# Down-projection of a seven-product gated MLP: another bank order, weight sums moved into the sweep, the last sums issued behind the next norm

## The chip, the cores and the metric

The kernel is one program on one core of a Trainium2 chip. TensorE multiplies matrices into PSUM (eight banks of 128 x 512 float32), VectorE and ScalarE do elementwise work and read PSUM, GpSimd works on SBUF alone, and SyncE issues all the transfers here. Each engine runs its own queue in order, and engines wait for each other by semaphores. The metric is the device time of one execution in microseconds. The times shown are those of three runs and, apart from them, of one profiled execution.

## The reference

A two-layer decoder over 1024 positions of width 1024, all in float32. Each layer has a mixer and a gated MLP (`conv_ffn`) of inner width 2816; the first mixer is a recurrence with a state-space layer, the second is latent attention (`mla`).

```python
for layer in range(2):
    hn = rmsnorm(h, norm_mix_g[layer])
    h = h + (even_mixer(hn, ...) if layer % 2 == 0 else mla(hn, positions, ...))
    h = h + conv_ffn(rmsnorm(h, norm_ffn_g[layer]), ffn_w_in[layer], ffn_conv_w[layer],
                     ffn_conv_b[layer], ffn_w_out[layer])
return rmsnorm(h, final_norm_g)

def conv_ffn(hn, w_in, conv_w, conv_b, w_out):
    a, u = jnp.split(hn @ w_in, 2, axis=-1)
    a = causal_depthwise_conv_width_3(a, conv_w) + conv_b
    return (jax.nn.silu(a) * u) @ w_out
```

The change touches the end of `conv_ffn` and the norm and first projections of `mla`.

## The kernel before, in words

Every float32 product is made of three fast ones: both operands are split into a high part (ScalarE, line 130) and a remainder (VectorE, line 131), and `mm3` (lines 162 to 164) adds high times high, and the two mixed ones.

Both matrix products of the MLP are done by a scheme of Strassen's kind: the operands are cut into halves along rows and columns, sums and differences of these are formed, and seven products of half size take the place of eight.

**The sweep** (`ffn`). The inner width is swept in 22 column blocks of 128, numbered `f`. Each has seven products of 12 matmuls (12 = 4 slices of the inner dimension x 3), which go to three banks X, Y and Z of the block; from the third block on, banks are drawn in turn from a list (`bank()`, list 3, 0, 6, 4, 1, 7, 5, 2). ScalarE and VectorE read the banks between the products (`run`, `tail`); L914 and L935 are the VectorE reads of the product in Y and of the last one in Z. GpSimd forms the sums of the raw weights (L883 to L889). The gated result of each block, `ct`, is stored to DRAM (`g_dram`).

Blocks go in pairs, `q` = 0 to 10. After the second block of a pair, `tail` puts steps on the list `later`: four `row_sums` (sums of the pair's results, stored to `g_dram`) and, up to the last pair but one, a set of `weight_sums` of the same pair: two loads of 128 x 1024 of the output weights, three empty steps, four subtractions (L985), each stored to `t_dram` (L986). One step is taken after each product of the sweep. Both kinds work in the same two tiles (`homes`: q1 has the place of `gain`, q2 that of the last of three `wlo` tiles). The last pair's set and what is left are issued in `between`, after the first product of the down-projection.

**The down-projection** (`down`). Seven products of 132 matmuls each: 11 pairs `q` x 4 row blocks `t` x 3. Each product accumulates into four banks, one for a row block. X is the first four banks of the ring (0 to 3), Y the other four; later products reuse them. For each `q` a *unit* is made: a row tile is loaded (L1150 from `g_dram`, L1155 from `t_dram` or from the weights), then split on ScalarE and VectorE into one of the unit buffers: six pairs of halves in the places of the MLP's operands and four tiles of its own pool, 14 in all, or 10 for the last product, which leaves two large places free for the next norm. Row tiles go round ten places, one of them the place of q2. Units are asked for nine ahead. The last `tail` values of `q` are done row block by row block, so that the four banks end one after the other. `add` (L1180) then adds each bank to the residual rows `h`; each product feeds one or more quarters of `h`. The last product, number 6, feeds the second half's right quarter; the rows of the first half are complete one product earlier.

**The border to the attention layer** (`mla`). `norm_rows` squares the rows on ScalarE (L201), takes the reciprocal root on VectorE (L173 to L184, ten small operations for two rows), scales the rows (L205), transposes them on TensorE (L211, tiles `tps`) into banks tagged `t`, and splits them into `hn`. The low-rank projections (tile `low`) follow, with banks tagged `mm`. In the second MLP, `final` norms and stores each row block as it is completed.

**What sets the order.** The program is written in Python's order and a scheduler lays each engine's queue from a simulated timeline; `high_priority` and `issue_after` (an instruction issued no sooner than a given one) shape it. On the chip the queues stand as laid.

Of the kernel before, what the change touches and what calls it, by code (L numbers as in the profile page):

```python
# [27 lines left out]
NF = FF // P  # L28
# [14 lines left out]
HM = 5  # L43
FRAW, FW = 2, 0
LOOK = 3
EL, OL = (1, 2), (1, 3)
LASTMAJ, MB, FB = True, (2, 2), (1, 2)
SEQ = "s s k00 s s g0 s q00 r00 k02 r01 q02 s r02 s v1 r03 s o0 g1 s k10 q10 r10 k12 q12 r11 r12 r13"
# [8 lines left out]
class Trunk:  # L57
# [134 lines left out]
    def norm_rows(self, h, g, batch=4, tags=("hn", "hn")):  # L192

        nc = self.nc
        hi = self.slot(tags[0], [P, KD, HALF], F32R, name="hn_hi")
        lo = self.slot(tags[1], [P, KD, HALF], F32R, name="hn_lo")
        ss = self.small.tile([P, TB], F32, tag="ss", name="ss")
        for b0 in range(0, TB, batch):
            for t in range(b0, b0 + batch):
                junk = self.xp.tile([P, D], F32, tag=self.xtag, name="junk", bufs=2)  # L200
                nc.scalar.activation(junk, h[:, t], AF.Square, accum_out=ss[:, t:t + 1])  # L201
            r = self.rstd(ss[:, b0:b0 + batch], D, batch)
            for t in range(b0, b0 + batch):
                xn = self.xp.tile([P, D], F32, tag=self.xtag, name="xn", bufs=2)
                nc.vector.scalar_tensor_tensor(  # L205
                    out=xn, in0=h[:, t], scalar=r[:, t - b0:t - b0 + 1], in1=g, op0=ALU.mult, op1=ALU.mult
                )
                for q in range(2):
                    ps = self.bank(name="tps", tag="t")
                    for k in range(4):  # L210
                        nc.tensor.transpose(  # L211
                            ps[:, k * P:(k + 1) * P], xn[:, (4 * q + k) * P:(4 * q + k + 1) * P], self.ident
                        )
                    dst = lambda x: x[:, 4 * q:4 * q + 4, t * P:(t + 1) * P]
                    self.split(dst(hi), dst(lo), ps.rearrange("p (k n) -> p k n", k=4))
        return hi, lo
# [605 lines left out]
    def ffn(self, L, h, pool, final=None):  # L822


        nc, tc = self.nc, self.tc
        V, G, ACT = nc.vector, nc.gpsimd, nc.scalar
        self.xp, self.xtag = pool, "ct"
        w_in, w_out = self.a["ffn_w_in"][L], self.a["ffn_w_out"][L]
# [4 lines left out]
        g_dram, t_dram = (  # L833
            tc.dram_tile([NF // 2, n, P, HALF], F32, name=name) for n, name in ((7, "g_dram"), (4, "t_dram"))
        )
        KH = KD // 2
        last, later = [], []
        quad = [P, 2, KH, HALF]
        piece = lambda name, bufs: pool.tile([P, HALF], F32, tag=name, name=name, bufs=bufs)
        kn = lambda x: x.rearrange("p (k n) -> p k n", k=KH)  # L840
# [92 lines left out]
        def tail(p):  # L933
            ct = p.ct
            V.tensor_tensor(out=p.p16, in0=p.p16, in1=p.Z, op=ALU.add)  # L935
            V.tensor_tensor(out=ct[:, lo], in0=ct[:, lo], in1=p.X, op=ALU.mult)
            G.tensor_tensor(out=ct[:, hi], in0=ct[:, hi], in1=p.p16, op=ALU.mult)
            q, odd = p.f // 2, p.f % 2
            put = lambda i, x: nc.sync.dma_start(out=g_dram[q, i], in_=x)
            put(odd, ct[:, hi])  # L940
            if not odd:
                return
            put(2, ct[:, lo])
            later.extend(row_sums(q, pairs[p.f - 1].ct, ct))
            if p.f < NF - 1:
                later.extend(weight_sums(q))

        def homes():
            return (
# [24 lines left out]
        def weight_sums(q):  # L974

            x = []

            def load():
                for i, y in enumerate(homes()):
                    nc.sync.dma_start(out=y, in_=w_out[(2 * q + i) * P:(2 * q + i + 1) * P])  # L980
                    x.extend((y[:, lo], y[:, hi]))

            def step(i, out, a, b):
                def go():
                    V.tensor_tensor(out=x[out], in0=x[a], in1=x[b], op=ALU.subtract)  # L985
                    nc.sync.dma_start(out=t_dram[q, i], in_=x[out])  # L986
                return go

            wait = lambda: None
            return [load, wait, wait, wait, step(0, 0, 1, 0), step(2, 1, 3, 1), step(1, 3, 3, 0), step(3, 2, 2, 3)]  # L990

        two = lambda tag, name: (lambda v: (v[:, 0], v[:, 1]))(self.slot(tag, quad, F32R, name=name))
        single = lambda tag, name, dtype=F32R: pool.tile([P, KH, HALF], dtype, tag=tag, name=name, bufs=1)
# [97 lines left out]
        for i, (p, name) in enumerate(steps):  # L1091
            if i + LOOK < len(steps):
                prep(*steps[i + LOOK])
            for x, first in (("X", "a11"), ("Y", "s2"), ("Z", "s1")):
                if name == first:
                    setattr(p, x, here(p.banks[x]) if p.f < 3 else bank())
            run(p, name)
            if later:
                later.pop(0)()
            left[p.f] -= 1  # L1100
            if not left[p.f]:
                tail(p)

        self.psum(mm=8)
        later.extend(weight_sums(NF // 2 - 1))

        def between():
            while later:
                later.pop(0)()
            return final() if final is not None else None  # L1110

        self.down(h, g_dram, t_dram, w_out, between)

    def conv(self, out, ax, taps, f, span):

# [6 lines left out]
            nc.vector.scalar_tensor_tensor(out=t, in0=at(s), scalar=col(s), in1=t, op0=ALU.mult, op1=ALU.add)  # L1122
        nc.scalar.activation(t, t, AF.Silu)

    def down(self, h, g, turned, w, between):


        nc, tc = self.nc, self.tc
        V = nc.vector
        nq = NF // 2  # L1130
        low = [(x, n) for tag, k in (("hn", 2), ("g", 3)) for x in [tag] * k for n in range(2)]
        own = [(f"b{i}", 0) for i in range(2, 6)]
        units = {True: low + own, False: low[4:] + own}
        held, at, last = {}, [0], []

        def unit(free):
# [24 lines left out]
        def product(banks, a, b, start, free, tail):  # L1161
            us = []
            order = [(q, t) for q in range(nq - tail) for t in range(TB)]
            order += [(q, t) for t in range(TB) for q in range(nq - tail, nq)]
            for q, t in order:
                while len(us) < min(nq, q + 9):
                    us.append(operands(len(us), a, b, free))
                u = us[q]
                with tc.issue_after(last[0].ins) if last else nullcontext():
                    mm = self.mm3(  # L1170
                        banks[t], [u[:, i, 0, t * P:(t + 1) * P] for i in range(2)], [u[:, i, 1] for i in range(2)],
                        start and q == 0, q == nq - 1, skip_group_check=not start,
                    )
                last[:] = [mm]

        def add(banks, *to, done=()):
            for t in range(TB):
                for half, col in to:
                    x = h[half][:, t, col * HALF:(col + 1) * HALF]
                    V.tensor_tensor(out=x, in0=x, in1=banks[t], op=ALU.add)  # L1180
                for half, col in done if final is not None else ():
                    final(h[half], half, t, col)
# [12 lines left out]
        X = banks()  # L1195
# [2 lines left out]
        product(Y, 2, 3, False, True, 3)  # L1198
        add(Y, (0, 0), done=[(0, 0), (0, 1)])
        at[0] = 0  # L1200
        product(X, 6, (1, 1), False, False, 7)
        add(X, (1, 1), done=[(1, 1)])

    def project_rows(self, h, x, w, tags=("mm",) * TB, late=1):

# [101 lines left out]
        nc.gpsimd.tensor_tensor(out=d[:, :, 0], in0=pc[:, :, 0], in1=ps[:, :, 1], op=ALU.subtract)  # L1307
        nc.vector.tensor_tensor(out=d[:, :, 1], in0=pc[:, :, 1], in1=ps[:, :, 0], op=ALU.add)

    def mla(self, h, keep, pool):  # L1310
        nc, tc, a = self.nc, self.tc, self.a
        NT = S // P
        w_in = a["odd_w_in"][0]
# [3 lines left out]
        ka = keep.tile([P, S], F32R, name="ka", bufs=1)  # L1317
        kb = keep.tile([P, S], F32R, name="kb", bufs=1)
        with pool("mla_in") as tp, self.weights(0, 5, 768), pool("norm", "right") as self.xp:
            self.psum(mm=6, t=2)  # L1320
            self.xtag = "xn"
            g_row = self.gain(a["norm_mix_g"][1:2])
            gains = {}
# [4 lines left out]
            for half in range(2):  # L1328
                with tc.high_priority():
                    tags = ("hn", "hn") if half == 0 else ("h", "g")  # L1330
                    hn.append(self.norm_rows(h[half], g_row, batch=MB[half], tags=tags))
                    for t in range(TB):
                        nc.sync.dma_start(out=spill[half][:, t], in_=h[half][:, t])
            cos, sin = self.rope_tables(tp)
            cq = [self.slot("g", [P, QR // P, S], F32R, name=n) for n in ("cq_hi", "cq_lo")]
            ck = self.slot("h", [P, 2, KVR // P, S], F32R, name="ckv")
# [291 lines left out]
def trunk(tc, a, out, parts=("mix0", "ffn0", "mix1", "ffn1")):  # L1628
    with ExitStack() as ctx:
        T = Trunk(ctx, tc, a, out)  # L1630
        pool = lambda n, side="left": tc.tile_pool(name=n, bufs=2, reuse_waits="tile", side=side)
        first_g = []
        start = lambda: first_g.append(T.gain(a["norm_mix_g"][0:1])) if parts[0] == "mix0" else None
        h = [T.load_rows(0, start), None if parts[0] == "mix0" else T.load_rows(1)]
        for part in parts:
            if part == "mix0":
                T.psum(mm=4, s5=1, s5p=1, t=2)
                with T.weights(), pool("hgrn") as hp:
                    h = T.even(h, first_g[0], hp, pool, lambda n: pool(n, "right"), lambda: pool("mix_out"))
            elif part == "mix1":  # L1640
                with pool("mla") as keep:
                    h = T.mla(h, keep, pool)
            else:
                L = int(part[3])
                T.psum(mm=6, t=2)
                with T.weights(FRAW, FW), pool(part, "right") as fp:
                    T.ffn(L, h, fp, final=(lambda: T.final(fp)) if part == parts[-1] else None)


INS = [  # L1650
# [24 lines left out]
```

## Time and profile before

| | us |
|---|---|
| median of three runs (2300.55 to 2304.01) | 2301.92 |
| profiled execution | 2303.47 |
| its span, first to last instruction | 2301.8 |
| TensorE busy in it | 2206.0 |
| VectorE busy | 1648.9 |
| ScalarE busy | 925.4 |
| GpSimd busy | 553.7 |

Mean granted TensorE clock: 0.985 of full speed. The first MLP's sweep runs from about 485 to 913, its down-projection to 1136, the attention layer to about 1620, the second MLP's sweep from there to 2069 and its down-projection to 2293. In what follows PE is TensorE, PEld its weight loads, DVE VectorE, ACT ScalarE, POOL GpSimd and SP SyncE. A wait is idle time of an engine, put down to the instruction that ended it.

### The profile page before, as it was taken

The numbers are of one execution on the slowest core, as the hardware profiler recorded it, in microseconds if no ns is written. First come the engines' busy times: TensorE is split into PE (matmuls) and PEld (weight loads), VectorE is DVE, ScalarE is ACT, GpSimd is POOL, SyncE is SP. The second block draws the span as 40 slices with busy tenths as digits, with TensorE's granted clock in tenths as the row PEclk, the third lists the DMA queues.
The fourth block names the chain that finished last, engine by engine and source line by source line (L and its number), as shares of the span: only waits on it lengthen the run. The fifth ranks groups of instructions, "written<-read, shape, count | busy, mean of one in ns | idle before, by whom it ended". The sixth has DMA issues, their size and how long they took to land. (4 is left out here: it accounts for less than half of the span.)

```text
span 2301.8 us, 30062 instructions
## 1 busy us (share of the span) xinstructions
PE 2206.0 (96%) x10681; PEld 1815.2 (79%) x10681; DVE 1648.9 (72%) x2749; ACT 925.4 (40%) x1564; POOL 553.7 (24%) x509
## 2 busy tenths in 40 slices
PE   7999999999999999899799999999999999999998
PEld 6777887877777887788698888888777878877786
DVE  6778896698777777654467677766887777777556
ACT  4454544443333334342243555544533333333432
POOL 0365510125444442100001000000344444431000
PEclk9999999999999999999999999999999999999999
DMA  6432333415444446864311001054144444558642
GB/s 188 136 99 87 99 92 109 139 37 173 152 148 159 146 164 228 288 201 131 128 31 43 28 22 39 29 179 137 37 156 160 141 166 136 180 197 293 206 155 82
DMA packets 257214, 306.18 MB, mean 133 GB/s; under 512 B 35680, under 2 KB 159784, under 8 KB 256552
## 3 DMA queue, kind: packets, MB, share of 16 engines
q1 hardware_dynamic: 257064, 304.26, 40.2%
q8 instruction: 84, 1.38, 0.3%
q14 instruction: 66, 0.54, 0.1%
HBM read 223.06 MB, written 79.95 MB: 132 GB/s over the span
## 5 line engine op out<-in xcount | busy, mean ns | idle before, releaser
L162 PE MATMUL au<-bt,op 128*128 128x512 f32 x704 | 280.8, 399 | 15.7 <-DVE p L914 8.5
L131 DVE TENSOR_TENSOR unit<-row,unit 128x1024 fp32r<-128x1024 f32 x154 | 185.5, 1233 | 149.2 <-ACT unit L130 136.8
L163 PE MATMUL au<-bt,op 128*128 128x512 f32 x704 | 278.9, 396 | 1.2 <-DVE bt L131 1.2
L164 PE MATMUL au<-bt,op 128*128 128x512 f32 x704 | 278.8, 396 | 0.0
L130 ACT ACTIVATE op<-raw 128x512 fp32r<-128x512 f32 x260 | 161.7, 627 | 254.2 <-PE au L164 123.3
L162 PE MATMUL row<-unit 128*128 128x512 f32 x616 | 243.8, 396 | 18.4 <-ACT unit L130 10.3
L130 ACT ACTIVATE unit<-row 128x1024 fp32r<-128x1024 f32 x154 | 155.6, 1053 | 255.6 <-PE row L164 166.9
L131 DVE TENSOR_TENSOR op<-raw,op 128x512 fp32r<-128x512 f32 x260 | 217.3, 838 | 56.7 <-ACT op L130 56.3
L163 PE MATMUL row<-unit 128*128 128x512 f32 x616 | 243.2, 395 | 2.1 <-DVE unit L131 2.1
L164 PE MATMUL row<-unit 128*128 128x512 f32 x616 | 242.8, 394 | 0.0
L164 PE MATMUL au<-b,op 128*128 128x512 f32 x528 | 208.6, 395 | 1.1 <-DVE op L131 1.1
L162 PE MATMUL au<-b,op 128*128 128x512 f32 x528 | 208.5, 395 | 0.0
L163 PE MATMUL au<-b,op 128*128 128x512 f32 x528 | 208.4, 395 | 0.0
L162 PEld LDWEIGHTS au<-bt,op 128*128 128x128 f32 x704 | 132.6, 188 | 56.2 <-DVE p L914 14.0
L131 DVE TENSOR_TENSOR wlo<-raw,whi 128x1024 fp32r<-128x1024 f32 (+4 forms) x99 | 118.1, 1194 | 62.5 <-ACT whi L130 61.8
L163 PEld LDWEIGHTS au<-bt,op 128*128 128x128 f32 x704 | 132.9, 189 | 32.5 <-DVE bt L131 1.5
L164 PEld LDWEIGHTS au<-bt,op 128*128 128x128 f32 x704 | 132.8, 189 | 31.9
L130 ACT ACTIVATE whi<-raw 128x1024 fp32r<-128x1024 f32 (+4 forms) x99 | 96.7, 980 | 141.9 <-PE row L164 63.2
L162 PEld LDWEIGHTS row<-unit 128*128 128x128 f32 x616 | 117.6, 191 | 45.0 <-ACT unit L130 11.2
L163 PEld LDWEIGHTS row<-unit 128*128 128x128 f32 x616 | 117.6, 191 | 28.5 <-DVE unit L131 3.5
L164 PEld LDWEIGHTS row<-unit 128*128 128x128 f32 x616 | 117.3, 190 | 25.0
L883 POOL TENSOR_TENSOR s<-raw 128x512 f32<-128x512 f32 x44 | 63.1, 1436 | 267.1 <-DMA raw<-in_ffn_w_in 231.8
(599 smaller groups left out, 5081.5 us busy)
## 6 DMA issues: line engine op xcount, KB each, us to landing
raw<-in_ffn_w_in SPq DMA_DIRECT2D x176, 256.0 KB, 3.4
row<-g_dram SPq DMA_DIRECT2D x154, 256.0 KB, 4.0
g_dram<-q SPq DMA_DIRECT2D x88, 256.0 KB, 3.7
q<-in_ffn_w_out SPq DMA_DIRECT2D x44, 512.0 KB, 4.1
t_dram<-q SPq DMA_DIRECT2D x88, 256.0 KB, 2.1
row<-t_dram SPq DMA_DIRECT2D x88, 256.0 KB, 4.2
raw<-in_even_w_in SPq DMA_DIRECT2D x40, 512.0 KB, 3.7
g_dram<-ct SPq DMA_DIRECT2D x66, 256.0 KB, 2.1
```

Source lines behind the costliest of these rows:

```text
L130: nc.scalar.activation(hi, src, AF.Copy)
L131: nc.vector.tensor_tensor(out=lo, in0=src, in1=hi.bitcast(F32), op=ALU.subtract)
L162: mm(out, l[0], r[0], start=start, stop=False, **how)
L163: mm(out, l[0], r[1], start=False, stop=False, **how)
L164: return mm(out, l[1], r[0], start=False, stop=stop, **how)
L883: tt(out=s.s1, in0=p("a21"), in1=p("a22"), op=ALU.add)
```

## The change

Four edits, for both MLPs unless said:

- The down-projection's banks come from a list, 0, 4, 1, 6, 7, 5, 2, 3, instead of 0 to 7. The attention layer's norm and projections take their banks from lists, too.
- Sets of weight sums are put on the list after blocks 5, 7, 9 (two), 11, 13 (two), 15, 17 (two) and 19, all eleven of them in the sweep; each ends with one more empty step, and two steps are taken after a product while more than 14 wait.
- Units are asked for as far ahead as there are buffers less one. The last product of the first MLP has only the six units in the large places, and its last three values of `q` are done row block by row block instead of the last seven.
- The last product's `add` is handed back as a function. In the second MLP it is called at once; in the first it is called inside the attention layer, after the norm of the first half, and not ahead of that norm's last scaling.

```diff
+TURNS = {5: 1, 7: 1, 9: 2, 11: 1, 13: 2, 15: 1, 17: 2, 19: 1}
...
-                nc.vector.scalar_tensor_tensor(
+                self.scaled = nc.vector.scalar_tensor_tensor(
...
             later.extend(row_sums(q, pairs[p.f - 1].ct, ct))
-            if p.f < NF - 1:
-                later.extend(weight_sums(q))
+            for _ in range(TURNS.get(p.f, 0)):
+                later.extend(weight_sums(turned[0]))
+                turned[0] += 1
...
-            return [load, wait, wait, wait, step(0, 0, 1, 0), step(2, 1, 3, 1), step(1, 3, 3, 0), step(3, 2, 2, 3)]
+            return [load, wait, wait, wait, step(0, 0, 1, 0), step(2, 1, 3, 1), step(1, 3, 3, 0), step(3, 2, 2, 3), wait]
...
-            if later:
-                later.pop(0)()
+            for _ in range(1 + (len(later) > 14)):
+                if later:
+                    later.pop(0)()
...
-        self.psum(mm=8)
-        later.extend(weight_sums(NF // 2 - 1))
+        self.rings = {"mm": [[0, 4, 1, 6, 7, 5, 2, 3], 0]}
...
-        units = {True: low + own, False: low[4:] + own}
+        units = {True: low + own, False: low[4:] + (own if last_layer else [])}
...
-                while len(us) < min(nq, q + 9):
+                while len(us) < min(nq, q + len(units[free]) - 1):
...
-        product(X, 6, (1, 1), False, False, 7)
-        add(X, (1, 1), done=[(1, 1)])
+        product(X, 6, (1, 1), False, False, 7 if last_layer else 3)
+        return lambda: add(X, (1, 1), done=[(1, 1)])
...
-            self.psum(mm=6, t=2)
+            self.rings = {"mm": [[2, 3, 0, 4, 1, 6], 0], "t": [[7, 5], 0]}
...
                     for t in range(TB):
                         nc.sync.dma_start(out=spill[half][:, t], in_=h[half][:, t])
+                if half == 0:
+                    with tc.issue_after(self.scaled.ins):
+                        rest()
```

The queue of transfers (SP) at the start of the first MLP's down-projection, around the last row sums, before. `q` tiles are the two homes, L980 and L986 the loads and stores of a weight set:

```order
L964 DMA g_dram<-q_7900 128x512
L980 DMA q_7909<-in_ffn_w_out 128x1024
L1150 DMA row<-g_dram 128x512 x2
L1155 DMA row<-in_ffn_w_out 128x512
L980 DMA q_7910<-in_ffn_w_out 128x1024
L986 DMA t_dram<-q_7909 128x512
L1150 DMA row<-g_dram 128x512
L1155 DMA row<-in_ffn_w_out 128x512
```

The same place now, after the last row sum (lines have moved by two to four):

```order
L966 DMA g_dram<-q_7912 128x512
L1154 DMA row<-g_dram 128x512
L1159 DMA row<-in_ffn_w_out 128x512
L1154 DMA row<-g_dram 128x512
L190 DMA gain<-in_norm_mix_g 128x1024
L1154 DMA row<-g_dram 128x512
L1159 DMA row<-t_dram 128x512
```

The weight set that stood between the row loads is gone; the next thing on this queue that is no row load is the gain of the next norm.

VectorE's queue at the border, before: `h<-h,row` are the additions, `v` and `vy` the reciprocal root of the norm:

```order
L1180 TENSOR_TENSOR h<-h,row 128x512
L131 TENSOR_TENSOR unit<-row,unit 128x1024 x4
L1180 TENSOR_TENSOR h<-h,row 128x512 x4
L173 TENSOR_SCALAR v _9166<-ss 128x2
L1271 TENSOR_TENSOR ang<-freq,pos 128x8x32
L174 TENSOR_SCALAR vy<-v _9166 128x2
```

And now, from the end of the first half's norm on (`wlo` are weights of the projections, `hn_lo` the transposed rows):

```order
L206 SCALAR_TENSOR_TENSOR xn<-h,vy,gain 128x1024 x2
L132 TENSOR_TENSOR wlo<-raw,whi 128x640
L1184 TENSOR_TENSOR h<-h,row 128x512
L132 TENSOR_TENSOR wlo<-raw,whi 128x640
L1184 TENSOR_TENSOR h<-h,row 128x512
L132 TENSOR_TENSOR hn_lo<-tps,hn_hi 128x4x128
L1184 TENSOR_TENSOR h<-h,row 128x512
L132 TENSOR_TENSOR hn_lo<-tps,hn_hi 128x4x128
L1184 TENSOR_TENSOR h<-h,row 128x512
L174 TENSOR_SCALAR v _9271<-ss 128x2
```

The four additions of the last product stood ahead of the whole norm; they stand behind the first half's last scaling now, and ahead of the second half's root.

TensorE's queue at the end of the last product (`row<-unit`) before:

```order
L162 MATMUL row<-unit 128x512
L163 MATMUL row<-unit 128x512
L164 MATMUL row<-unit 128x512
L211 MATMUL tps<-ident,xn 128x128 x8
L162 MATMUL low<-whi,hn_hi 128x384
L163 MATMUL low<-wlo,hn_hi 128x384
```

And now, 51 matmuls into that product:

```order
L163 MATMUL row<-unit 128x512
L164 MATMUL row<-unit 128x512
L165 MATMUL row<-unit 128x512
L212 MATMUL tps<-ident,xn 128x128 x8
L163 MATMUL row<-unit 128x512
L164 MATMUL row<-unit 128x512
L165 MATMUL row<-unit 128x512
```

The first transposes of the norm stood behind the whole product; three of the first half's four groups of eight stand inside it now, after 51, 85 and 121 of its 132 matmuls.

## Rows read from the trace of the kernel before

**Rows 1.** Page, span and part 1: busy us, share of the span, instructions

```profile
span 2301.8 us, 30062 instructions
PE 2206.0 (96%) x10681; PEld 1815.2 (79%) x10681; DVE 1648.9 (72%) x2749; ACT 925.4 (40%) x1564; POOL 553.7 (24%) x509
```

**Rows 2.** Windows: length, busy (instructions) by engine, PEclk, DMA share, GB/s

```profile
910.00:920.00 10.00, 6.69 (x29) 5.16 (x28) 8.33 (x9) 7.83 (x9) 0.83 (x1) 1.00 1.03 376
965.00:985.00 20.00, 13.12 (x45) 9.91 (x45) 7.92 (x8) 5.69 (x6) 0.00 (x0) 0.74 0.69 239
990.00:1090.00 100.00, 100.00 (x442) 82.63 (x441) 48.91 (x47) 34.64 (x34) 0.53 (x2) 1.00 0.53 173
2065.00:2080.00 15.00, 10.20 (x34) 7.83 (x34) 12.42 (x12) 11.33 (x13) 2.04 (x2) 0.77 0.91 327
2125.00:2140.00 15.00, 10.34 (x33) 7.64 (x32) 6.48 (x7) 5.17 (x5) 0.00 (x0) 0.77 0.77 245
```

**Rows 3.** Windows of 5 us at the border to the attention layer

```profile
1135.00:1140.00 5.00, 0.83 (x4) 0.36 (x2) 2.42 (x8) 0.00 (x0) 0.00 (x0) 1.00 0.57 183
1140.00:1145.00 5.00, 0.00 (x0) 0.00 (x0) 4.16 (x15) 1.15 (x2) 0.00 (x0) 0.58 0.55 157
1145.00:1150.00 5.00, 1.72 (x8) 1.57 (x8) 4.29 (x7) 1.91 (x4) 0.00 (x0) 0.50 0.47 131
1150.00:1155.00 5.00, 4.00 (x17) 3.71 (x16) 3.14 (x9) 4.97 (x10) 0.00 (x0) 0.55 0.45 131
...
1180.00:1185.00 5.00, 1.20 (x12) 0.99 (x10) 5.00 (x24) 1.08 (x2) 0.00 (x0) 1.00 0.00 2
1185.00:1190.00 5.00, 4.43 (x16) 4.13 (x15) 4.71 (x16) 1.13 (x2) 0.00 (x0) 0.52 0.32 105
1190.00:1195.00 5.00, 5.00 (x29) 4.96 (x29) 1.21 (x2) 1.09 (x2) 0.00 (x0) 0.80 0.00 0
```

**Rows 4.** TensorE's waits, 885 to 1210: total us, times, longest

```profile
PE tps L211 <- DVE xn L205: 16.3, 2, 12.5
PE row L162 <- ACT unit L130: 6.4, 1, 6.4
PE row L162 <- DVE p L935: 3.3, 1, 3.3
```

**Rows 5.** TensorE's waits, 2060 to 2302

```profile
PE row L162 <- DVE p L935: 4.8, 1, 4.8
PE row L162 <- ACT unit L130: 3.9, 1, 3.9
```

**Rows 6.** Timeline of the DMA queue: start, us, queue, line, transfer

```profile
949.79 0.33 SPq L986 DMA_DIRECT2D t_dram<-q  x1
...
962.33 1.46 SPq L986 DMA_DIRECT2D t_dram<-q  x1
963.84 2.63 SPq L1155 DMA_DIRECT2D row<-t_dram  x2
```

**Rows 7.** Timeline of VectorE at the border

```profile
1135.87 0.69 DVE L1180 TENSOR_TENSOR h<-h,row 128x512 f32<-128x512 f32 x1 [4.13 <-PE row L164]
1136.47 0.16 DVE L173 TENSOR_SCALAR v _9166<-ss 128x2 f32<-128x2 f32 x1
...
1146.95 2.48 DVE L205 SCALAR_TENSOR_TENSOR xn<-h,vy,gain 128x1024 f32<-128x1024 f32 x2
```

**Rows 8.** Timeline of ScalarE at the border

```profile
1112.17 1.04 ACT L201 ACTIVATE junk<-h 128x1024 f32<-128x1024 f32 x1
```

**Rows 9.** Window: the first 110 us of the first sweep

```profile
500.00:610.00 110.00, 104.64 (x444) 82.43 (x443) 91.39 (x109) 33.48 (x52) 52.61 (x42) 1.00 0.46 151
```

**Rows 10.** VectorE's groups, 500 to 900: busy us, mean ns, idle before

```profile
L985 DVE TENSOR_TENSOR q<-q,q 128x512 f32<-128x512 f32 x20 | 18.8, 940 | 0.9 <-DMA q<-in_ffn_w_out 0.9
...
L985 DVE TENSOR_TENSOR q<-q 128x512 f32<-128x512 f32 x20 | 14.3, 714 | 34.0 <-DMA q<-in_ffn_w_out 34.0
```

**Rows 11.** Page, part 5: a group of GpSimd's sums in the sweep

```profile
L883 POOL TENSOR_TENSOR s<-raw 128x512 f32<-128x512 f32 x44 | 63.1, 1436 | 267.1 <-DMA raw<-in_ffn_w_in 231.8
```

More of the change, by code (lines that the diff above doesn't have):

```diff
@@ L836, in ffn @@
         KH = KD // 2
-        last, later = [], []
+        last, later, turned = [], [], [0]
         quad = [P, 2, KH, HALF]
@@ L1110, in between @@
             return final() if final is not None else None
-        self.down(h, g_dram, t_dram, w_out, between)
+        return self.down(h, g_dram, t_dram, w_out, between, final is not None)
     def conv(self, out, ax, taps, f, span):
@@ L1123, in conv, with down @@
         nc.scalar.activation(t, t, AF.Silu)
-    def down(self, h, g, turned, w, between):
+    def down(self, h, g, turned, w, between, last_layer):
         nc, tc = self.nc, self.tc
@@ L1308, in rotate, with mla @@
         nc.vector.tensor_tensor(out=d[:, :, 1], in0=pc[:, :, 1], in1=ps[:, :, 0], op=ALU.add)
-    def mla(self, h, keep, pool):
+    def mla(self, h, rest, keep, pool):
         nc, tc, a = self.nc, self.tc, self.a
@@ L1641, in trunk @@
                 with pool("mla") as keep:
-                    h = T.mla(h, keep, pool)
+                    h = T.mla(h, rest, keep, pool)
             else:
@@ L1646, in trunk @@
                 with T.weights(FRAW, FW), pool(part, "right") as fp:
-                    T.ffn(L, h, fp, final=(lambda: T.final(fp)) if part == parts[-1] else None)
+                    rest = T.ffn(L, h, fp, final=(lambda: T.final(fp)) if part == parts[-1] else None)
+                    if part == parts[-1]:
+                        rest()
 INS = [
```

## The prediction

> **What bounds the kernel now.** The page comes first: TensorE is busy for 2206.0 us of a span of 2301.8 [rows 1]. It is the engine that sets the time, and only stretches in which it stands still, or runs at half clock, can give anything back. The profiled execution took 2303.47 us, 1.67 beside its span; the three timed runs have a median of 2301.92, which is 1.55 less. I make the sum against 2303.47 and take 1.55 off at the end.
>
> Second, the pace. In an undisturbed stretch of the down-projection 442 matmuls of 512 columns start in 100 us at a granted clock of 1.00: 0.2262 us each [rows 2]. What a stretch of such matmuls lost is its length less its matmuls at that pace. Around the two starts of a down-projection and inside the second product:
> - 910 to 920: 10 − 29 × 0.2262 = 3.4 us
> - 965 to 985: 20 − 45 × 0.2262 = 9.8
> - 2065 to 2080: 15 − 34 × 0.2262 = 7.3
> - 2125 to 2140: 15 − 33 × 0.2262 = 7.5
>
> Where shapes are mixed, I take the length less busy time times granted clock [rows 3]. From 1135 to 1155, the border between the first gated MLP and the attention layer: 20 − (0.83 + 0 + 1.72 × 0.50 + 4.00 × 0.55) = 16.1. From 1180 to 1195: 15 − (1.20 + 4.43 × 0.52 + 5.00 × 0.80) = 7.5. The six places together: 51.6 us. Half of that is clock: the wait itself in the stretch from 2125 is 3.9 us [rows 5], and the stretch lost 7.5.
>
> Third, the waits of TensorE by what ended them [rows 4, 5]. The first product of a down-projection waits for the addition at L935 (3.3 and 4.8 us): its fourth bank is 3, the bank of the last column block's last product, which that addition reads. The second product waits for a converted unit (6.4 and 3.9 us), and the transposes at the border wait for the scaled rows (16.3 in two waits).
>
> **The change part by part.**
>
> *Banks in order of release.* The ring of the sweep gives the last column block (21) banks 6, 7, 0 of its list, that is X=5, Y=2, Z=3; block 20 has 4, 1, 7; block 19 has 3, 0, 6. The new list begins 0, 4, 1, 6: all four are read for the last time by blocks 19 and 20. No instruction is added; eight more matmuls of the first product stand ahead of the sweep's last two products. What is late next is the fifth unit of that product, which TensorE reaches 34 matmuls, 7.7 us, after the end of the sweep. Both places go (3.4 and 7.3); I leave 0.3 each for what is late next: −10.1.
>
> *Weight sums all in the sweep.* The eleventh set (two loads, four subtractions, four stores) no longer stands at the start of the down-projection. On the DMA queue before, its stores go out between 949.79 and 962.33, each holding the row loads behind it, and the loads of the turned weights that the end of the second product needs are issued only from 963.84 on, over 2.63 us [rows 6]; TensorE stands from 967 on. Without it that load waits for nothing younger than the sweep. The loads may also run 13 units ahead instead of 9, so units are nearer in time than row buffers, of which one is no longer held by a weight set. Bounds: all of 9.8 + 7.5, or nothing if the row buffers were the true limit. I take 17.3 less 0.5 each: −16.3.
>
> In the sweep the sets now skip the first two pairs and come doubled after blocks 9, 13 and 17. The first 110 us of the first sweep have 5.4 us without TensorE, while VectorE is busy for 91 of them [rows 9]; two sets leave there, and the second layer's sweep is built alike. One set is 4 × about 0.8 us of VectorE [rows 10]. I give back 2.0 a layer for these and charge 0.8 for each of three doubled sets: +0.4 a layer, +0.8. From below: twice the 5.4 us go, 10.8. From above: the wait for the loads, 34.0 us over ten sets on VectorE [rows 10], is 3.4 a set, now without four steps between load and use where two steps are taken at a time; if TensorE sees all of it for six sets, +20.
>
> One rule speaks against this part. GpSimd works in the sweep, 1436 ns for one of its sums [rows 11], and the same VectorE subtraction of one size averages 714 ns in one form and 940 in the other there [rows 10], so some of them wait. The Trainium skill, "SBUF — State Buffer", "Who interferes with whom", says that a VectorE operation with two inputs in SBUF and a GpSimd operation reading SBUF exclude each other, the later one standing until the other ends. The trace agrees that far. By the row, a moved set costs 2 × 0.226 = 0.45 us more, which lies within the 0.8; by the rule at its worst each of the four waits for a whole GpSimd sum, 4 × 1.436 × 2 layers = 11.5 us if TensorE saw all of it, and the time would be 2267. I keep the row.
>
> *Last product's sums behind the next norm.* At the border the four additions of the last product stand on VectorE's queue before the rows' reciprocal root, so the norm of the first half, whose rows were complete 30 us earlier, starts at 1136.47, and its first scaled rows come at 1146.95 [rows 7]. Its squares had long run, at 1112 [rows 8]. In the new order the reciprocal root and the scaling stand ahead of the additions, and the transposes of three of the four row blocks stand inside the last product, 51, 85 and 121 matmuls after its start: 11.5, 20 and 30 us. The chain from the root to the scaled rows took 10.5 us before with other work in between and 2.48 us for two scalings [rows 7]; started about 2 us before the product itself, it is done 11 us into it at the latest. The 24 transposes move, they don't add: they run in the product instead of behind it. The last row block follows the product among the projections, and their weights need eight loads through two buffers, which now fall into the last 25 us of the product. The norm of the second half starts as the last additions end, about 34 us after the product's start; its first transposes stand some 46 matmuls of the projections later, about 8 us, and need the same ten-odd us of which three are already past. I leave 1.0 at the first place and 1.5 at the second: −(16.1 + 7.5 − 2.5) = −21.1.
>
> The last product of that layer has six units of buffer instead of ten, because its own-pool tiles must be free for the norm. A unit lasts 12 matmuls, 2.7 us, so five ahead are 13 us of cover; at nothing, unless ScalarE's queue holds a unit behind a weight conversion.
>
> The rest of the attention layer is ordered a little differently with the same instructions; TensorE has no idle to win there. At nothing; −2 to +4.
>
> Sum: 10.1 + 16.3 − 0.8 + 21.1 = 46.7. 2303.47 − 46.7 − 1.55 = 2255.
>
> **Rivals.**
>
> *The last product starves.* Units 8 to 10 stand behind conversions of the next layer's weights on ScalarE, and these wait for loads; or the second pair of scaled rows is late and TensorE stands in the middle of the product. For it: the chain is within a microsecond or two of the transposes. Against: the reordered queue puts six units ahead of the first weight. Price: a stop like the one at 1180, 7.5 us: 2263.
>
> *The second product still waits.* The saturated transfers (DMA share 1.03 at 910 to 920 [rows 2]) and not the weight sums make the units late. Against: from 990 to 1090 the share is 0.53 at full pace. Price 16.3: 2271.
>
> *Doubled sets stop the sweep.* Six times 3.4 less the 2.4 × 2 already charged: +15.6, 2271.
>
> *Slower.* The two tiles that hold a set are single; the second load of a double waits for the first set's stores, and all loads share one queue. If the queue stands so long that the next blocks' input weights are late, TensorE waits at six places. It decides when each costs more than 46.7 / 6 = 7.8 us beyond the two-pair lead of these loads; at 9 us each the time is 2309. A store to DRAM held the queue for 1.46 us [rows 6], so far less.
>
> **How the numbers follow.** Forecast, 2255 (2248 to 2261 with its own bounds): 0.62. Starving last product 0.15; second product still late 0.10; doubled sets 0.09; slower 0.02; the remaining 0.02 is more gain than summed, all the idle of the early sweeps (2246). The range 2247 to 2272 leaves out under 2 in 10. 0.2% is 4.6 us, about what a measurement of this kernel can tell from no change. All cases but one are far below that: faster 0.97, same 0.01, slower 0.02.
>
> **What would show it.** No wait of TensorE for L936 (the old L935) at the start of either down-projection; no wait for a unit 22 us into the second product, and granted clock 1.00 through both; transposes inside the last product with no idle ahead of them; at the border one continuous run of TensorE at 1.00. The doubled sets would show as VectorE idle for the weight loads, with TensorE waits behind L915 (the old L914). The prediction is wrong if the border keeps more than 8 us, if the second product still stops, or if the sweep loses more than 5 us in one layer.

## The result and the profile after

The changed kernel took 2260.97 us in the median (2260.79 to 2261.14), the kernel before 2301.3 beside it: a ratio of 0.9823, interval [0.9806, 0.984], so 1.6 to 1.9% faster. The forecast was 2255, range 2247 to 2272. Direction and range held, and the time came out 6 us above the forecast. The profiled execution took 2260.85.

The page of the kernel after, span and part 1, against [rows 1]:

```profile
span 2259.1 us, 30081 instructions
PE 2192.1 (97%) x10681; PEld 1802.8 (80%) x10681; DVE 1661.3 (74%) x2749; ACT 926.0 (41%) x1564; POOL 560.8 (25%) x509
```

Windows of the kernel after: in each layer the start of the down-projection (the sweeps end at 915.6 and 2042.9) and its second product, and in the first layer the last product with the border behind it, against [rows 2, 3]; columns as there.

```profile
910.00:920.00 10.00, 10.00 (x45) 8.14 (x44) 6.34 (x7) 6.04 (x7) 1.85 (x1) 1.00 0.93 318
955.00:985.00 30.00, 30.00 (x134) 24.85 (x133) 22.12 (x23) 13.72 (x14) 0.00 (x0) 1.00 0.87 302
1092.00:1200.00 108.00, 108.00 (x642) 101.32 (x641) 74.63 (x192) 48.36 (x103) 5.06 (x4) 1.00 0.24 76
2040.00:2055.00 15.00, 15.00 (x68) 12.32 (x67) 14.08 (x14) 12.25 (x13) 1.00 (x1) 1.00 0.93 324
2080.00:2120.00 40.00, 40.00 (x178) 33.06 (x177) 26.02 (x25) 16.66 (x17) 0.00 (x0) 1.00 0.82 277
```

All six places run without idle at granted clock 1.00 (the third line holds both of the border). The only wait of TensorE listed from 890 to 1210, against [rows 4], is this:

```profile
PE lps L1400 <- DVE low L1395: 1.4, 1, 1.4
```

At the border VectorE's timeline, against [rows 7], has root and scaling ahead of the last product's additions (L1184):

```profile
1090.74 0.17 DVE L174 TENSOR_SCALAR v _9160<-ss 128x2 f32<-128x2 f32 x1 [1.22 <-ACT junk L202]
...
1098.36 2.48 DVE L206 SCALAR_TENSOR_TENSOR xn<-h,vy,gain 128x1024 f32<-128x1024 f32 x2
...
1120.21 0.68 DVE L1184 TENSOR_TENSOR h<-h,row 128x512 f32<-128x512 f32 x1
...
1126.12 0.16 DVE L174 TENSOR_SCALAR v _9271<-ss 128x2 f32<-128x2 f32 x1
```

and TensorE's timeline has the transposes inside that product, which begins at 1092.7, with no idle ahead of them:

```profile
1104.28 1.03 PE L212 MATMUL tps<-ident,xn 128*128 128x128 f32 x8
1112.88 1.03 PE L212 MATMUL tps<-ident,xn 128*128 128x128 f32 x8
1121.93 1.03 PE L212 MATMUL tps<-ident,xn 128*128 128x128 f32 x8
```

What is missing of the forecast went in the sweeps. TensorE's waits over the whole kernel before, those of the sweep:

```profile
PE au L162 <- DVE p L914: 8.5, 12, 1.4
PE au L162 <- DVE u L918: 2.7, 5, 0.9
```

and after:

```profile
PE au L163 <- DVE p L915: 12.7, 19, 2.2
PE au L163 <- DVE u L919: 8.3, 8, 2.4
```

Windows of the first sweep after: the early part of [rows 9], and the blocks with the doubled sets.

```profile
500.00:610.00 110.00, 107.64 (x460) 85.70 (x459) 91.42 (x104) 35.05 (x54) 56.09 (x45) 1.00 0.38 124
610.00:690.00 80.00, 80.00 (x345) 64.51 (x344) 61.62 (x80) 25.93 (x41) 33.26 (x28) 1.00 0.47 155
690.00:885.00 195.00, 187.53 (x794) 148.14 (x794) 150.38 (x192) 59.54 (x95) 80.64 (x66) 1.00 0.53 174
```

The same stretch before:

```profile
690.00:885.00 195.00, 194.54 (x834) 156.27 (x833) 148.53 (x190) 63.67 (x100) 84.04 (x70) 1.00 0.47 155
```

The idle of the early part shrank from 5.4 to 2.4 us, and from 690 to 885 it grew from 0.5 to 7.5.

To see this by place, I number the matmuls of a sweep (the transposes among them not counted) and take when the n-th starts, counted from the sweep's first, less the same in the kernel before. Loss in us (minus: ahead); block 6 begins at number 504, block 11 at 924, block 21 at 1764:

```
               first sweep                    second sweep
               0-504  924-1764  whole       0-252  252-504  924-1764  whole
after           -3.9     9.2      7.0         3.7    -3.7     10.1     11.5
e1_banks         0.7     0.7      3.3        -0.5     0.3     -0.1      1.8
e2_sums         -3.9     9.7      5.7        -0.6    -3.4      9.5      6.2
e3_border       -0.2     0.8      0.3         3.8     0.7      0.5      4.5
e4_single        0.7     4.0      6.7         3.5     1.7      3.6     10.0
e5_pool         -3.9    22.4     24.0         3.8    -3.7     20.1     24.7
e6_look9        -3.3    11.6     10.5         3.4    -3.4      9.6     10.9
e7_twos         -3.9    11.1      9.2         3.4    -3.4     10.7     12.0
e8_noload       -4.4     9.2      6.4         3.3    -3.4     11.6     12.2
after_again     -3.8    11.1      9.3         3.4    -3.4     10.4     12.0
e9_nosub        -4.7     7.7      4.8         3.3    -3.4      6.1      7.8
e10_conv        -5.6     9.2      5.3         1.7    -3.4     10.3      9.3
e11_conv_single -1.3     3.1      3.3         1.5     2.9      4.0      9.2
```

With the new banks 8 more matmuls of the down-projection (1.8 us) stand inside "whole". The down-projection by halves of a product (66 matmuls; 15.0 us is full pace): 1a is the first half of product 1, with those of its matmuls that stand inside the sweep counted at full pace, and 2b the second half of product 2. For layer 0, the first MLP, also the time from the first to the last matmul of the last product, and from there to the second sweep's first:

```
            layer 0:  1a    2b   last   to sweep 2     layer 1:  1a    2b
before               18.6  25.1  29.9     486.0                 22.4  22.9
e1_banks             15.0  28.4  29.9     487.8                 15.0  28.4
e2_sums              23.2  15.0  29.9     484.8                 21.7  15.0
e3_border            20.4  23.3  32.4     459.0                 22.0  22.0
after                15.0  15.0  32.4     459.2                 15.0  15.0
```

### The profile page after: what moved, and what is told of

The parts are those of the page before. It is cut to its first block, busy times and chain, and to the rows that moved or that the text cites. A ratio compares the mean times of both kernels' runs of the same rounds, so it can differ in the third digit from the quotient of the medians.

```text
span 2259.1 us, 30081 instructions
## 1 busy us (share of the span) xinstructions
PE 2192.1 (97%) x10681; PEld 1802.8 (80%) x10681; DVE 1661.3 (74%) x2749; ACT 926.0 (41%) x1564; POOL 560.8 (25%) x509
## 5 line engine op out<-in xcount | busy, mean ns | idle before, releaser
L132 DVE TENSOR_TENSOR op<-raw,op 128x512 fp32r<-128x512 f32 x260 | 229.4, 884 | 56.1 <-ACT op L131 55.2
L164 PE MATMUL row<-unit 128*128 128x512 f32 x616 | 240.4, 390 | 0.4 <-DVE unit L132 0.3
L165 PE MATMUL row<-unit 128*128 128x512 f32 x616 | 240.1, 390 | 0.0
L163 PE MATMUL row<-unit 128*128 128x512 f32 x616 | 240.0, 390 | 0.0
L164 PEld LDWEIGHTS row<-unit 128*128 128x128 f32 x616 | 115.7, 188 | 25.7 <-DVE unit L132 1.5
L163 PEld LDWEIGHTS row<-unit 128*128 128x128 f32 x616 | 115.6, 188 | 24.3
L165 PEld LDWEIGHTS row<-unit 128*128 128x128 f32 x616 | 115.6, 188 | 24.2
```

Of the source, the lines that this page charges most:

```text
L132: nc.vector.tensor_tensor(out=lo, in0=src, in1=hi.bitcast(F32), op=ALU.subtract)
L163: mm(out, l[0], r[0], start=start, stop=False, **how)
L164: mm(out, l[0], r[1], start=False, stop=False, **how)
L165: return mm(out, l[1], r[0], start=False, stop=stop, **how)
```

## The experiments

**One part alone**, on the kernel before. `e1_banks`:

```
-        self.psum(mm=8)
+        self.rings = {"mm": [[0, 4, 1, 6, 7, 5, 2, 3], 0]}
```

> The kernel before with the bank list [0, 4, 1, 6, 7, 5, 2, 3] for the down-projection and nothing else. Theory (the parts of the change add up): both waits for L935 go, and the time falls by 10 us, to 2291; the second product's wait for a unit stays at its place. Rival (the bank is only the first of two things that the first product waits for, the other being its fifth unit): the wait turns into one for a unit, the time falls by 3 us or less, to 2298 or more.

2296.11, ratio 0.9982 [0.9971, 0.9994]: 4.8 us, between the two. The first product runs at full pace, but the wait for a unit grows. TensorE's waits in its two down-projections:

```profile
PE row L162 <- ACT unit L130: 10.1, 1, 10.1
...
PE row L162 <- ACT unit L130: 10.0, 1, 10.0
```

Against 6.4 and 3.9 before: of the 11.0 us won at 1a, 8.8 come back at 2b. The size is nearer the rival's, by another wait than it named, some 50 us later.

`e2_sums`: TURNS, the double pop, the deeper prefetch and no set at the down-projection.

> The kernel before with the weight sums of the change (all eleven sets in the sweep, three of them doubled, the deeper prefetch of units) and nothing else. Theory (the doubled sets cost the sweeps about 15 us, the down-projections win 17): from its first matmul on au to its last, the first sweep takes 455 to 459 us where it took 450, the second 456 to 459 where it took 447, and the time falls by only 1 to 6 us, to 2295 to 2300. Rival (the sweeps' loss belongs to another part, such as the banks of its last products): the sweeps keep 450 and 447, and the time falls by 16 us, to 2285.

2296.58, ratio 0.9986 [0.9977, 0.9996]. The mirror image: 2b is free, the wait for the bank stays, 5.6 and 4.0 us (3.3 and 4.8 before); of the 18.0 us won at 2b, 3.9 are lost at 1a. The sweeps took 456.2 and 453.3; the second missed the 456 expected, since its start did not slip.

`e3_border`: the deferred `rest`, six units and a tail of three, bank lists [6, 7, 0, 1, 2, 3] and [4, 5] in the attention layer.

> The kernel before with the border of the change (last additions behind the next norm's scaling, six units and a tail of three in that product, bank lists for the attention layer that free the other half of the banks first) and nothing else. Theory: the border's two stretches go nearly whole, minus 21 to 25 us: 2276 to 2280. Rival (the norm can only start early because the product starts early and its units run ahead in the changed kernel): TensorE still stops for 5 us or more around the transposes, 2284 or more.

2276.75, ratio 0.9903 [0.9888, 0.9918]: 24 us, as the theory said. It also shows a cost: the second sweep loses 3.8 us in its first three blocks. At 1580 to 1665 the kernel before waits

```profile
PE au L162 <- DVE b L131: 1.3, 1, 1.3
```

and e3_border

```profile
PE au L162 <- DVE b L131: 2.3, 1, 2.3
PE au L162 <- DVE u L918: 1.3, 1, 1.3
```

In e3_border the second half's transposes stand ten matmuls later in TensorE's queue than in the kernel before. VectorE waits 1.6 us for them (0.6 in e1_banks), and its first addition behind them starts 17.2 us into the sweep, 14.8 in e1_banks. Whether all of the 3.8 us comes from this isn't shown.

Alone the three parts give 4.8, 4.3 and 24.1 us, 33.2 together; the change gave 40.3. The first two help each other: alone they win 2.2 and 14.1 us at 1a and 2b, together 29.0.

**Which of the two edits freed the second product**, on the changed kernel. `e6_look9`:

```
-                while len(us) < min(nq, q + len(units[free]) - 1):
+                while len(us) < min(nq, q + (9 if free else len(units[free]) - 1)):
```

> The changed kernel with units prepared 9 ahead in the first six products, as before, instead of 13. Theory (the second product's stop went because no weight set is left for the start of the down-projection): no change, 2259 to 2263. Rival (it went because units run further ahead): the stop of 8 to 10 us in the second half of the second product comes back in both layers, 2275 to 2281.

2265.75 (ratio 0.9838 [0.9821, 0.9854]; the changed kernel took 2265.37 on another chip of the later runs), 2.8 above the expected band and far from the rival's. 2b stays at 15.0 in both layers: the weight sets' place did it.

**What a doubled set costs.** `e4_single`:

```
-TURNS = {5: 1, 7: 1, 9: 2, 11: 1, 13: 2, 15: 1, 17: 2, 19: 1}
+TURNS = {1: 1, 3: 1, 5: 1, 7: 1, 9: 2, 11: 1, 13: 1, 15: 1, 17: 1, 19: 1}
```

> The changed kernel with the eleven weight sets spread as one after each pair from block 1 on, and a second one only after block 9 (TURNS alone differs). Theory (doubled sets hold VectorE's queue, and the ones after 13 and 17 with their backlog cost 4 to 5 us a layer, of which the two early sets give back some 1.5): 2253 to 2257, with no wait of TensorE over 1 us in blocks 14 to 21. Rival (eleven sets in a sweep cost the same wherever they stand): 2260 to 2262.

2257.59, ratio 0.9818 [0.9804, 0.9833], 0.6 above the theory's band. The time can't decide, the table does: past block 11 single sets cost almost nothing and the one double some 3.5, with the pair behind it, but the early sets take back what skipping them had won (0.7 and 1.7 where the changed kernel has −3.9 and −3.7).

`e5_pool`: `G.tensor_tensor` for `V.tensor_tensor` in the weight sums.

> The changed kernel with the subtractions of the weight sums on GpSimd instead of VectorE. Theory (a doubled set costs TensorE 3 us because it stands in VectorE's queue, ahead of the additions that free banks): the three losses of a sweep after its doubled sets, 9 us a layer, fall below 3: 2245 to 2252. Rival (GpSimd, at 1.3 to 1.4 us an operation and standing for the load in its turn, delivers its own sums late, and products wait for operands instead): 2261 or more.

2295.95, ratio 0.9973 [0.9959, 0.9988]: the theory fell badly, and the rival's reason too, though its time held, since TensorE waits for VectorE's L915 still (38.6 us). VectorE's groups from 500 to 900 in the changed kernel, mean ns after the busy time:

```profile
L1124 DVE SCALAR_TENSOR_TENSOR ct<-ax,taps,ct 128x1024 f32<-128x1024 f32 x42 | 54.7, 1303 | 0.4
L915 DVE TENSOR_TENSOR p<-p,au 128x512 f32<-128x512 f32 x20 | 13.6, 680 | 0.8 <-PE au L165 0.7
```

and in e5_pool, with the moved subtractions:

```profile
L1124 DVE SCALAR_TENSOR_TENSOR ct<-ax,taps,ct 128x1024 f32<-128x1024 f32 x40 | 65.8, 1645 | 0.6
L915 DVE TENSOR_TENSOR p<-p,au 128x512 f32<-128x512 f32 x20 | 13.6, 681 | 0.6 <-PE au L165 0.5
...
L987 POOL TENSOR_TENSOR q<-q,q 128x512 f32<-128x512 f32 x20 | 35.1, 1756 | 9.1 <-DMA q<-in_ffn_w_out 8.5
```

The mean of VectorE's operation with two inputs in SBUF rose by 342 ns, that of the one with an input in PSUM not at all. The mean is of two kinds of executions, though. By line, min, median and max in ns, the operation with two full-size inputs (L1124) and the first of the convolution, with one (L1122), in the changed kernel:

```profile
L1124 DVE SCALAR_TENSOR_TENSOR ct<-ax,taps,ct x42: 1267/1278/2309, 511.4 to 898.4; 128x1024 f32<-128x1024 f32 x42
L1122 DVE TENSOR_SCALAR ct<-ax,taps x21: 800/802/1784, 509.6 to 894.6; 128x1024 f32<-128x1024 f32 x21
```

and in e5_pool:

```profile
L1124 DVE SCALAR_TENSOR_TENSOR ct<-ax,taps,ct x40: 1269/1285/2312, 511.5 to 893.3; 128x1024 f32<-128x1024 f32 x40
L1122 DVE TENSOR_SCALAR ct<-ax,taps x20: 800/1766/1790, 509.7 to 889.2; 128x1024 f32<-128x1024 f32 x20
```

Of the 40 of L1124, 15 took 2.25 us in the mean, and each of these began while a GpSimd operation ran; the other 25 didn't, and took 1.28. In the changed kernel one of 42 was long. This agrees with the rule of the Trainium skill that the prediction weighed ("SBUF — State Buffer", "Who interferes with whom"). But L1122, with one full-size input, splits the same way, 13 of 20 at 1.78 us and 7 at 0.80, which the rule for two inputs alone doesn't give.

`e7_twos`: one entry per product; in doubled pairs `twos(s)` joins the steps.

> The changed kernel with one entry of the list taken per product everywhere; for the three doubled pairs the steps are joined two by two, so that both sets and the row sums fill exactly the 14 products of the pair. Theory (what a doubled set costs is the load of the second set used too soon and a backlog that makes the next pair's entries go out by twos): the losses after blocks 9, 13 and 17, some 3 us each, fall to 1 or less: 2246 to 2252. Rival (what costs is eight more VectorE operations within one pair, however they are spaced): 2258 to 2262.

2267.04, ratio 0.9843 [0.9828, 0.9858], above both. No gain: the losses past block 11 stay, 11.1 and 10.7, so this spacing is not it.

`e8_noload`:

```
-                    nc.sync.dma_start(out=y, in_=w_out[(2 * q + i) * P:(2 * q + i + 1) * P])
...
-                    V.tensor_tensor(out=x[out], in0=x[a], in1=x[b], op=ALU.subtract)
+                    V.tensor_tensor(out=x[out], in0=h[0][:, 0, :HALF], in1=h[1][:, 0, :HALF], op=ALU.subtract)
```

> The changed kernel without the loads of the weight sums: their subtractions take rows of h instead, at the same size, and the stores stay. It leaves out what the sums are made of. Theory (VectorE standing for the second load is most of the price of a doubled set): losses after blocks 9, 13 and 17 fall from 9.3 to 3 us a layer or less: 2246 to 2251. Rival (the number of VectorE operations is the price, not the wait): 2257 to 2261.

2258.23, ratio 0.9808 [0.9788, 0.9829], in the rival's band. The losses past block 11 stay, 9.2 and 11.6: taking the wait for the load away is not enough. It isn't a clean test of that wait, since the subtractions got longer. From 690 to 885:

```profile
L986 DVE TENSOR_TENSOR q<-h 128x512 f32<-128x512 f32 x27 | 27.1, 1039 | 6.0 <-DMA g_dram<-q 6.0
```

In after_again they are two groups of 814 and 687 ns in the mean there.

`after_again`, the yardstick of the last group:

> The changed kernel once more, as the yardstick of this group on its chip: 2259 to 2263, the sweeps losing some 5 and 11 us against the kernel before as they did.

2265.37, ratio 0.9839 [0.9823, 0.9854], 2.4 above the expected band; the interval overlaps the first one.

`e9_nosub`: the second set of each doubled pair without its `V.tensor_tensor`.

> The changed kernel with the four subtractions of the second set of each doubled pair left out (24 in all); loads and stores stay, so for three of the eleven column pairs the rows stored are the loaded weights instead of their differences. Theory (the price of a doubled set is its four VectorE operations in a stretch where VectorE keeps up with one per product and not with two): the losses after blocks 9, 13 and 17 fall from 9.3 us a layer to 3 or less, 12 us or more below the changed kernel of this group. Rival (it is the transfers of the set, which hold the queue of the next blocks' weights): 0 to 4 us below.

2258.11, ratio 0.9806 [0.9789, 0.9822]: 7.3 below, between the two. The losses fall from 11.1 and 10.4 to 7.7 and 6.1, so over the whole stretch leaving them out gains some 4 us of about 10.5 a layer. What VectorE waits for from 690 to 885, in the kernel before:

```profile
DVE q L985 <- DMA q<-in_ffn_w_out: 17.2, 6, 4.7
...
DVE u L918 <- PE au L164: 9.5, 9, 1.4
```

in the changed kernel (after_again):

```profile
DVE q L987 <- DMA q<-in_ffn_w_out: 26.4, 11, 4.2
...
DVE u L919 <- PE au L165: 1.6, 2, 0.9
```

and without these subtractions:

```profile
DVE q L988 <- DMA q<-in_ffn_w_out: 17.8, 4, 5.9
DVE q L965 <- DMA t_dram<-q: 11.5, 3, 4.6
```

By place the gain is larger. Loss against the kernel before in us, of the three pairs of blocks that begin with 10, 14 and 18, in which the doubled sets are worked off, and of the two that begin with 12 and 16:

```
               first sweep              second sweep
               10, 14, 18    12, 16     10, 14, 18    12, 16
after_again        8.3         2.3          7.0         2.9
e8_noload          7.1         2.1         10.3         1.3
e9_nosub          -0.1         7.1         -0.4         4.5
```

Without the second set's subtractions the pairs with the doubled sets lose nothing, though its loads and stores are still there; without the loads they lose as much as ever. So the price of a doubled set in its own pair is its subtractions, and the theory was right there. What remains in e9_nosub is lost in the pairs behind. Just ahead of them, at the end of each doubled pair, VectorE stands for stores of the one pair of tiles that all sets and row sums share (L965 above), up to 4.6 us; that this makes the later loss is likely, not shown. A second pair of tiles would tell, and wasn't tried.

`e10_conv`:

```
-        nc.vector.tensor_scalar(out=t, in0=at(2), scalar1=col(2), scalar2=col(3), op0=ALU.mult, op1=ALU.add)
+        nc.scalar.activation(t, at(2), AF.Identity, scale=col(2), bias=col(3))
```

> The changed kernel with the first of the three convolution operations of each block on ScalarE instead of VectorE. Theory (VectorE's queue is what the sweeps pay): 0.95 us a block leaves VectorE, more than the 3.1 us of a doubled set in every two pairs, and the sweeps' losses after doubled sets fall by half or more: 8 to 18 us below the changed kernel of this group. Rival (the convolution's chain gets longer by the hand-over between engines, and ScalarE's operand conversions come later): 0 to 10 us above.

2258.6, ratio 0.9802 [0.9787, 0.9817]: 6.8 below, just short of the 8 expected, and not by the way expected. The sweeps won 4.0 and 2.7 us, most of it outside the blocks of the doubles, which still cost 9.2 and 10.3 (11.1 and 10.4 beside it), though VectorE has an operation of 1.05 us a block less to do (the mean of 44 in the changed kernel, where the expectation had 0.95). Its wait for the product that L919 reads is back at what it was before the change, from 690 to 885:

```profile
DVE u L919 <- PE au L165: 9.1, 8, 1.4
```

So work taken from VectorE elsewhere in the block didn't pay for the subtractions. Whether it matters where in the block they stand, no run here tells.

`e11_conv_single`: e10_conv with the TURNS of e4_single.

> As the kernel with the convolution's first operation on ScalarE, and with one weight set after each pair from block 1 on, doubled after block 9 alone. Theory: with VectorE relieved neither the early sets nor the doubled one cost TensorE what they did (3.9 to 4.6 and 3.5 us a layer): 12 to 20 us below the changed kernel of this group. Rival (early sets meet the start of the sweep, where other work of VectorE is due): within 4 us of the kernel with the convolution on ScalarE and the sets of the change.

2253.86, ratio 0.9788 [0.9773, 0.9802]: 11.5 below the changed kernel beside it, in the interval clear of it and the best of all. The theory missed its near end by half a microsecond, and in its reason: the early sets still cost 4.3 and 6.3 us (−1.3 and 2.9 against −5.6 and −3.4 of e10_conv), and what went are two doubles a layer (3.1 and 4.0 left of 9.2 and 10.3).

## Why the prediction was right, and where it was off

By the two profiled executions, in us of span (−42.7 in all; the forecast's sum was −46.7):

- **Banks and weight sums at the down-projection**: forecast −26.4, measured 3.6 + 10.1 + 7.4 + 7.9 = −29.0 (1a and 2b in the table). Right together. Split as −10.1 and −16.3 it was wrong: alone, banks win 2.2 there, because the time saved at the first stop is waited at the second. The weight sums alone won 14.1, as the first stop got longer. The two terms may only be added because both stops go.
- **Border**: forecast −21.1, measured 486.0 + 29.9 − 459.2 − 32.4 = 24.3, so −24.3. The root starts 2.0 us ahead of the last product (forecast about 2), and the transposes begin 11.6, 20.2 and 29.2 us into it (11.5, 20 and 30). The reserves of 2.5 were not needed. The product does not starve on six units.
- **Sweep**: forecast +0.8, measured +5.2 and +9.7 (7.0 and 11.5 less 1.8 each), +14.9. This term failed, and by the sign that the prediction set itself (more than 5 us lost in one layer) it was wrong in both. It went in three places. Skipping the early sets won some 4 us a layer, not 2.0. The doubled sets cost 9.2 and 10.1 a layer, 3.1 to 3.4 each, where I charged 0.8, the length of one subtraction, although the bound beside it was the wait for a set's loads, 3.4 [rows 10], and the total lay near it: +20 for six, 19.3 measured. The size agrees with that bound, but not the reason: e8_noload has no loads and the same loss, and e9_nosub, with the loads but without the second set's subtractions, loses nothing in the doubled pairs. The wait for GpSimd's sums that the prediction priced at 11.5 isn't the reason either: the subtractions of [rows 10], 940 and 714 ns before, average 870 and 702 in the changed kernel (lines below). And the rewritten order behind the border costs 4 us at the second sweep's start; the forecast had "−2 to +4" for the attention layer, counted at nothing, and looked no further.
- **Unchanged code**: the kernel after reached the first sweep 4.4 us sooner (457.9 against 462.3 at the same matmul), with the same instructions in the same order. e1_banks, e2_sums and e3_border, equally unchanged there, came at 458.5 to 459.4: the profiled execution of before was a late one. Between the two profiles the forecast's sum was 4 us too large; without this, which is luck, it would have been 8.

The subtractions in the changed kernel, 500 to 900, against [rows 10]:

```profile
L987 DVE TENSOR_TENSOR q<-q,q 128x512 f32<-128x512 f32 x22 | 19.2, 870 | 6.7 <-DMA q<-in_ffn_w_out 6.6
L987 DVE TENSOR_TENSOR q<-q 128x512 f32<-128x512 f32 x22 | 15.5, 702 | 29.1 <-DMA q<-in_ffn_w_out 29.1
```

So the third rival (doubled sets stop the sweep) was true in its price, beside the forecast and not instead of it: it had 15.6 more than charged, and 19.3 − 4.8 = 14.5 came. Larger gains than forecast gave some of this back, 2.6 at the down-projections, 3.2 at the border and 3.6 from the early sets. That the time still came out within 6 us of the forecast is in part luck: errors of the other sign met this one.

## What to carry to other kernels

Two stops in a row can share their time: here removing the first alone moved 8.8 of 11.0 us to the second, so try them as a pair before believing either term. An engine that is busy three quarters of a stretch need not have room, and its waits for the bounding engine don't settle it either: VectorE waited 9.5 us for the product that L918 reads from 690 to 885 before and 1.6 in after_again, but 9.1 in e10_conv, where the doubled sets cost as much. What settled it was to take out the operations alone and the transfers alone, and to look where in the sweep the loss went, not only at its sum. An order made anew by a scheduler can cost far from the edit, here 450 us later; compare the whole trace by counted instructions, not only the places of the change.

## What the runs showed that was not expected

Moving 4 × 11 subtractions a layer from VectorE to a GpSimd that was busy for 41% of the time from 690 to 885 made the kernel 31 us slower than the changed kernel beside the later runs: one took 1.6 to 1.8 us there, and 15 of 40 executions of a VectorE operation on two SBUF inputs, those begun while GpSimd worked, took 2.25 us in place of 1.28.
